# Stacking the low part of the attention's queries twice in a diffusion block on one core

## The chip, the cores and the metric

The kernel runs on one core of one Trainium2 chip. The metric is the device time of one execution in microseconds. Three runs of the kernel before took 866.24, 866.44 and 866.78 us; the median, 866.44 us, is the time that the prediction starts from.

## The reference

One layer of a hybrid backbone block is computed in float32 for 512 latent tokens (a grid of 8 rows by 64 columns), 256 context tokens and a model width of 1024. One combined projection feeds four mixers (pooling, Fourier, Hyena, neighbourhood attention), each 256 channels wide; their outputs are projected, gated, summed and projected again, and a gated feed-forward part follows. The change touches the scores of the neighbourhood attention alone:

```python
    s_nb = jnp.einsum('brqhd,brikhd->bhrqik', q, kb).astype(jnp.float32) * scale + bias
    s_cx = jnp.einsum('brqhd,bchd->bhrqc', q, kc).astype(jnp.float32) * scale
    ...
    s = jnp.concatenate([s_nb.reshape(B, NA_HEADS, rows, GRID_W, n_nb), s_cx], axis=-1)
    prob = jax.nn.softmax(s, axis=-1).astype(v.dtype)
```

There are 4 heads of 64 channels. A query sees a window of 8 rows by 16 columns of the grid and all 256 context keys.

## The kernel before

Everything lies with channels on the 128 partitions and tokens on the free axis, save in the attention. Nearly all products run in a one-pass float32 format of TensorE (F32R) that keeps fewer bits; so that no accuracy is lost, each operand is split into a high part and a low part (`split`, lines 95 to 97: ACT copies to the high part, DVE subtracts it from the original for the low part), and a product is the sum of three matmuls, high by high, high by low, low by high (`mm3`, lines 99 to 102). Weights arrive by DMA from the SP queue in chunks and are split the same way (`load_split`, line 84).

The attention (lines 846 to 931) goes by units. A unit is one block of 16 columns (128 queries) of one head; there are 16 of them, u = 0 to 15. `scores` (line 852) runs the score products of a unit into two PSUM tiles, `psl` (neighbourhood keys, 256 or 384 columns) and `psc` (256 context keys), and has the softmax done by DVE and ACT: DVE adds the bias and takes the maxima (`sl`, `mx`), ACT takes exponentials (`pr`), DVE scales `pr`. `turn` (line 884), one unit later, transposes `pr` on TensorE (PSUM tiles `ptl`, `ptc`), and `values` (line 897), for two units together in every second one, multiplies by v (PSUM tile `pav`). The PSUM tiles named `psl`, `psc`, `ptl`, `ptc`, `pav` and `ppool` share four buffers under one tag (`ps`, line 74). Between the units runs `step` (line 915), one of the 24 merge steps of the other three branches: 24 matmuls of 512 columns for the gate (`pin`), 6 for the branch (`pbr`), one split of a weight chunk (`wgh` on ACT, `wgl` on DVE) and a sum on DVE (`sg`, `macc`). `mod_rest` (line 839) adds work for DVE alone (`wm`), fed by a DMA into two buffers.

The operands of the scores are built by `stack` (line 714), once for heads 0 and 1 ahead of the pooling branch, and once for heads 2 and 3 from inside `scores`. A head has 64 channels, half of the array's 128 rows. `stack` puts the high part of q into both halves of `qs`, and the high and the low part of k into the two halves of `ks` (and `kcs` for the context keys). One matmul of all 128 rows so gives high by high plus high by low. The third product, low part of q by high part of k, takes a second matmul, of the 64 rows that `own` names: lines 865 and 867.

The program text is not the order on an engine: the framework's planner orders the instructions of each engine ahead of time by its own estimate of their costs, except in a stretch at the start that is pinned. Each engine then runs its list in that order.

Of the kernel before, what the change touches and what calls it, by code (L numbers as in the profile page):

```python
# [8 lines left out]
F32 = mybir.dt.float32  # L9
# [37 lines left out]
def block_kernel(ctx: ExitStack, tc: tile.TileContext, A):  # L47
# [3 lines left out]
    # an engine whose instructions keep the program's order while pinned is set  # L51
# [104 lines left out]
    # the same, spread over the partitions (tokens on the free dimension)  # L156
# [9 lines left out]
    # the table of the square root, loaded ahead of its use  # L166
# [18 lines left out]
    with ExitStack() as mix:  # L185
# [22 lines left out]
        # =================== start: modulation, first norm, filters of hyena ===================  # L208
# [6 lines left out]
        with ExitStack() as st:  # L215
# [19 lines left out]
            # filters of hyena: the two sine layers  # L235
# [28 lines left out]
            # statistics of x: sums of squares on the tensor engine  # L264
# [19 lines left out]
            # sums and differences of the filters' two directions, for each t mod 4  # L284
# [3 lines left out]
            # the sum of both directions' magnitudes is the larger magnitude of their sum and difference  # L288
# [9 lines left out]
            def filt_abs(s):  # L298
                ab = vx[1 + s % 2]
                if s == 0:  # L300
                    V.tensor_tensor(hacc, ab[:, 0], ab[:, 1], ALU.max)
                    # the backward filter starts at the second tap
                    f0, f1 = hyp_[0:1, 0], hym_[0:1, 0]
                    G.tensor_tensor(f0, f0, f1, ALU.add)
                    G.tensor_scalar(f0, f0, 0.5, None, ALU.mult)
                    G.tensor_copy(f1, f0)
                else:
                    V.tensor_tensor(ab[:, 0], ab[:, 0], ab[:, 1], ALU.max)
                    V.tensor_add(hacc, hacc, ab[:, 0])
# [3 lines left out]
            # transform at the odd frequencies f < 128; from sums over t = 4 u + r for each r follow those of  # L313
            # f, 511 - f, 255 - f and 256 + f (the second and third with the sine part negated)
            def fold(j):
                if j == 0:
                    kst.extend(yslot("kst", dt=F32) for _ in range(4))
                kP, kM, kQ, kR = kst
                if j < 2:
                    src = (hyp_, hym_)[j]  # L320
                    pa, pb = ps("pKe"), ps("pKo")
                    for dst, q in ((pb, 2), (pa, 0)):
                        PE.matmul(dst, tabK[:, q, j], src[:, q], start=True, stop=True)
                    ob = sp.tile([P, T], F32, name="kob", tag="hm", bufs=3)
                    S.copy(ob, pb)
                    kpa[j] = pa, ob
                else:
                    # tabK's last part is that of t mod 4 = 3 negated
                    src, cs, q, dst = ((hyp_, 0, 3, kQ[:, 0]), (hym_, 1, 3, kQ[:, 1]),
                                       (hyp_, 1, 4, kR[:, 0]), (hym_, 0, 4, kR[:, 1]))[j - 2]  # L330
                    pa = ps("pKe")
                    PE.matmul(pa, tabK[:, 1, cs], src[:, 1], start=True, stop=False)
                    PE.matmul(pa, tabK[:, q, cs], src[:, 3], start=False, stop=True)
                    S.copy(dst, pa)
# [6 lines left out]
            # shift and scale of the first norm, channel tile by channel tile, for c and c_ctx  # L341
# [175 lines left out]
        # =================== input projection, hyena ===================  # L517
# [9 lines left out]
        # projections that run while hyena's transforms occupy the vector engine  # L527
# [23 lines left out]
        # v with tokens on the partitions, for x in blocks of 16 columns  # L551
# [48 lines left out]
        # one order of hyena: to the spectrum, product, first stage back  # L600
        def spectrum(o, z):
# [16 lines left out]
            # cosine and sine sums for each t mod 4, then those of the four frequencies that share them  # L618
# [21 lines left out]
            # product of the spectra  # L640
# [6 lines left out]
            # back: coefficients of cos and sin for t mod 4 = 0, 2, 1, 3  # L647
# [13 lines left out]
        # back to the tokens, skip, gate  # L661
# [49 lines left out]
        # q's high part twice, k's high and low part, one above the other: one pass has both products  # L711
        stacks = []

        def stack(ct):
            ql = ap_.tile([P, T], F32R, name="ql", tag="ql", bufs=1)
            for o in range(2):
                own, other = slice(o * 64, o * 64 + 64), slice(64 - o * 64, 128 - o * 64)
                qs = ap_.tile([P, T], F32R, name="qs", tag="qs", bufs=2)
                ks = ap_.tile([P, T], F32R, name="ks", tag="ks", bufs=2)
                kcs = ap_.tile([P, TC], F32R, name="kcs", tag="kcs", bufs=2)  # L720
                split(qs[own], ql[own], qt[own, ct])
                S.copy(qs[other], qt[own, ct])
                for st, src in ((ks, kt), (kcs, kc)):
                    S.copy(st[own], src[own, ct])
                    V.tensor_sub(st[other], src[own, ct], st[own].bitcast(F32))
                stacks.append((qs, ql[own], ks.rearrange("p (r x) -> p r x", r=8), kcs, own))

        # bias of each head, in the three forms that the columns' windows take
# [18 lines left out]
        # =================== pooling over windows of 2, 4 (first tile) and 8, 16 (second tile) ===================  # L747
# [5 lines left out]
        for c in range(2):  # L753
# [5 lines left out]
            # entry t of a sum over a window w covers t - w/2 .. t + w/2 - 1  # L759
# [19 lines left out]
        # =================== fnet ===================  # L779
        bd = yslot("bd", (P, TC), F32)  # L780
        nc.sync.dma_start(bd, A["bd"])
        # sums and differences of the tokens t and T - t, for even and odd t
# [10 lines left out]
        for e in range(2):  # L793
            tabF.append(xtile("tabF").rearrange("p (c k) -> p c k", c=2))
            nc.sync.dma_start(tabF[e], A["tabF"][:, e])
            p = ps("pucs")
            for c in range(2):
                for cs in range(2):
                    o = slice(c * TC + cs * P, c * TC + (cs + 1) * P)
                    PE.matmul(p[:, o], uft[:, c, 2 * e + cs], bd[:, cs * P:(cs + 1) * P], start=True, stop=e == 1 or cs == 0)  # L800
                    if e == 0 and cs == 1:
                        # the token T / 2, which has no partner, in the place of the sine part of t = 0
                        PE.matmul(p[:, o], mid[:, c], bd[:, 0:P], start=False, stop=True)
            ucs.append(xtile("ucs"))
            S.copy(ucs[e], p)
        yh_fn, yl_fn = yslot("yfh"), yslot("yfl")
        for c in range(2):
# [5 lines left out]
            # the even part plus and minus the odd part  # L813
# [6 lines left out]
        # =================== q, k, v, context ===================  # L820
        macc = [xtile("macc") for _ in range(KT)]

        def merge(b, jt, y):
            wh, wl = load_split(A["wg"][b * KT + jt], WCH, name="wg")
            p = projw(wh, wl)
            # a gate's sigmoid is (1 + tanh(x / 2)) / 2; the half goes into the sum's scale
# [12 lines left out]
        def mod_rest(t):  # L839
            # one column block of the modulation's other parts  # L840
            wm = mrp.tile([P, D], F32, name="wm2", tag="wm2", bufs=2)
            nc.sync.dma_start(wm, A["wmB"][t])
            V.tensor_tensor_reduce(wm, wm, cb, 1.0, 0.0, ALU.mult, ALU.add, modc[:, t:t + 1])


        # =================== attention, fnet, pooling, merge of the first branches ===================
        with at:
# [3 lines left out]
            # scores, their maximum, exponentials and sum  # L851
            def scores(ct, i, o):
# [8 lines left out]
                qs, ql, ks, kcs, own = stacks[h]  # L861
# [3 lines left out]
                PE.matmul(plv, ql[:, qc], ks[own, :, kw], start=False, stop=True)  # L865
                PE.matmul(pc[:, :TC], qs[:, qc], kcs, start=True, stop=False)
                PE.matmul(pc[:, :TC], ql[:, qc], kcs[own], start=False, stop=True)
# [15 lines left out]
            # keys on the partitions  # L883
# [12 lines left out]
            # product with v, two heads at a time  # L896
# [37 lines left out]
        # =================== last branch, merged sum ===================  # L934
# [11 lines left out]
        # =================== output projection ===================  # L946
# [28 lines left out]
        # the last tiles in halves of the tokens, so that the second norm starts ahead of their end  # L975
# [17 lines left out]
    # =================== feed-forward ===================  # L993
    with ExitStack() as ff:
# [25 lines left out]
        # the first tiles in halves of the tokens, two at a time  # L1020
# [191 lines left out]
```

## Time and profile before

| | |
|---|---|
| median of three runs | 866.44 us |
| span of the profiled execution | 864.0 us |
| TensorE matmuls busy | 843.5 us (98%) |
| TensorE weight loads busy | 685.5 us (79%) |
| DVE busy | 501.2 us (58%) |
| ACT busy | 333.1 us (39%) |
| POOL busy | 6.0 us (1%) |

The span runs from the first to the last instruction of one execution; 2.4 us of the median lie outside it. PE stands for TensorE's matmuls and PEld for its weight loads, which are instructions of their own. The ends of matmuls are modelled and overlap with the next ones, so a busy share says little of how fast the work goes: the distance from the start of one matmul to the start of the next does. In the rows below a row of the timeline gives start, length, engine, line, operation, output and inputs, the shape (rows of the array by columns of the array, then the moving operand), the count of merged instructions, and in brackets the idle time of the engine ahead of it with what ended it. Every line reads L60, because all instructions go through one helper there; the tiles' names tell them apart.

### The profile page before, as it was taken

The numbers are of one execution on the slowest core, as the hardware profiler recorded it, in microseconds if no ns is written. First come the engines' busy times: TensorE is split into PE (matmuls) and PEld (weight loads), VectorE is DVE, ScalarE is ACT, GpSimd is POOL, SyncE is SP. The second block draws the span as 40 slices with busy tenths as digits, with TensorE's granted clock in tenths as the row PEclk, the third lists the DMA queues.
The fourth block names the chain that finished last, engine by engine and source line by source line (L and its number), as shares of the span: only waits on it lengthen the run. The fifth ranks groups of instructions, "written<-read, shape, count | busy, mean of one in ns | idle before, by whom it ended". The sixth has DMA issues, their size and how long they took to land.

```text
span 864.0 us, 10732 instructions
## 1 busy us (share of the span) xinstructions
PE 843.5 (98%) x4192; PEld 685.5 (79%) x4192; DVE 501.2 (58%) x870; ACT 333.1 (39%) x519; POOL 6.0 (1%) x16
## 2 busy tenths in 40 slices
PE   6999999989999999999999999999999999999996
PEld 2577889777777778888888998888888888888886
DVE  4879997698797773444444774444444444233233
ACT  7544452625453342323333363333333333232321
POOL 0100000000000000000000000000000000000000
PEclk9999999999999999999999999999999999999998
DMA  8912214545555532223332222222222223223222
GB/s 315 414 50 74 98 43 162 164 168 180 195 183 183 199 137 92 91 92 116 124 126 98 73 89 108 98 98 98 98 98 98 98 94 95 86 92 91 86 68 98
DMA packets 30362, 107.30 MB, mean 124 GB/s; under 512 B 3783, under 2 KB 4935, under 8 KB 29288
## 3 DMA queue, kind: packets, MB, share of 16 engines
q1 hardware_dynamic: 30312, 106.62, 35.2%
q8 instruction: 33, 0.54, 0.2%
q14 instruction: 17, 0.14, 0.0%
HBM read 104.51 MB, written 2.10 MB: 123 GB/s over the span
## 4 chain that ended last, share of the span: by engine, by line
PE 86%; DVE 8%; ACT 2%; DMA 2%; issue 1%; SPq 0%; DVEq 0%; ACTq 0%
PE pup L60 28%; PE pin L60 25%; PE pdn L60 14%; PE pwo L60 5%; PE pbr L60 5%; PE psc L60 1%; DVE za L60 1%; PE pav L60 1%; PE pKe L60 1%; PE psl L60 1%; DVE winl L60 1%; DVE zb L60 1%; PE ptl L60 1%; DMA cb<-in_crow_dram 1%; PE pmod L60 1%
## 5 line engine op out<-in xcount | busy, mean ns | idle before, releaser
L60 PE MATMUL pup<-hxh,wupl 128*128 128x512 f32 (+1 forms) x376 | 140.8, 376 | 0.0
L60 PE MATMUL pup<-hxl,wuph 128*128 128x512 f32 (+1 forms) x376 | 140.6, 376 | 0.0
L60 PE MATMUL pup<-hxh,wuph 128*128 128x512 f32 (+1 forms) x376 | 139.9, 376 | 0.7 <-ACT wuph L60 0.4
L60 PE MATMUL pdn<-act,wdnh 128*128 128x512 f32 (+1 forms) x396 | 112.7, 368 | 0.0
L60 PE MATMUL pin<-hxh,wgh 128*128 128x512 f32 x256 | 101.4, 396 | 0.6 <-ACT wgh L60 0.6
L60 PE MATMUL pin<-hxh,wgl 128*128 128x512 f32 x256 | 100.5, 393 | 0.0
L60 PE MATMUL pin<-hxl,wgh 128*128 128x512 f32 x256 | 100.3, 392 | 0.0
L60 DVE TENSOR_TENSOR wupl<-wupr,wuph 128x1024 fp32r<-128x1024 f32 x44 | 53.9, 1225 | 71.5 <-ACT wuph L60 69.7
L60 ACT CAST wuph<-wupr 128x1024 fp32r<-128x1024 f32 x44 | 46.3, 1053 | 92.3 <-PE pup L60 86.3
L60 PEld LDWEIGHTS pdn<-act,wdnh 128*128 128x128 f32 x396 | 71.6, 189 | 12.0
L60 PEld LDWEIGHTS pup<-hxh,wuph 128*128 128x128 f32 x376 | 70.1, 188 | 13.8 <-ACT wuph L60 0.6
L60 PEld LDWEIGHTS pup<-hxh,wupl 128*128 128x128 f32 x376 | 70.7, 188 | 12.9 <-DVE wupl L60 0.2
L60 PEld LDWEIGHTS pup<-hxl,wuph 128*128 128x128 f32 x376 | 70.6, 188 | 12.9
L60 PE MATMUL pdn<-act,wdnl 128*128 128x512 f32 (+1 forms) x198 | 72.4, 366 | 0.0
L60 ACT ACTIVATE sg<-pin 128x512 f32<-128x512 f32 x32 | 19.2, 600 | 119.5 <-PE pin L60 119.5
L60 DVE TENSOR_TENSOR wdnl<-wdnr,wdnh 128x1024 fp32r<-128x1024 f32 (+1 forms) x24 | 27.2, 1134 | 63.2 <-ACT wdnh L60 63.1
L60 DVE SCALAR_TENSOR_TENSOR sg<-sg,pbr 128x512 f32<-128x512 f32 x24 | 16.5, 688 | 80.2 <-PE pbr L60 80.2
L60 PEld LDWEIGHTS pin<-hxh,wgh 128*128 128x128 f32 x256 | 48.1, 188 | 10.8 <-ACT wgh L60 1.0
L60 PEld LDWEIGHTS pin<-hxh,wgl 128*128 128x128 f32 x256 | 48.1, 188 | 10.5 <-issue 0.5
L60 PEld LDWEIGHTS pin<-hxl,wgh 128*128 128x128 f32 x256 | 48.1, 188 | 10.1 <-issue 0.5
L60 PE MATMUL pin<-hxh,winh 128*128 128x512 f32 x128 | 51.7, 404 | 0.0
L60 ACT CAST wdnh<-wdnr 128x1024 fp32r<-128x1024 f32 (+1 forms) x24 | 23.6, 982 | 72.4 <-PE pdn L60 66.7
(265 smaller groups left out, 1429.2 us busy)
## 6 DMA issues: line engine op xcount, KB each, us to landing
wupr<-in_wup_dram SPq DMA_DIRECT2D x44, 512.0 KB, 3.4
wgr<-in_wg_dram SPq DMA_DIRECT2D x32, 640.0 KB, 3.8
wm<-in_wmB_dram SPq DMA_DIRECT2D x32, 512.0 KB, 4.7
wm<-in_wmA_dram SPq DMA_DIRECT2D x8, 1024.0 KB, 10.7
winr<-in_win_dram SPq DMA_DIRECT2D x16, 512.0 KB, 3.5
wdnr<-in_wdn_dram SPq DMA_DIRECT2D x16, 512.0 KB, 3.4
wor<-in_wout_dram SPq DMA_DIRECT2D x8, 512.0 KB, 3.5
wdnr<-in_wdn_dram SPq DMA_DIRECT2D x8, 384.0 KB, 3.0
```

What stands on the lines that cost most here:

```text
L60: ins = f(*a, **k)
```

## The change

The low part of q becomes a tile like `qs`: a buffer for each head (two under the tag `ql` where there was one for a pair of heads), with the low part in both halves. `stack` makes two subtractions for a head where it made one; the copies on ACT stay two. The second product of each pair takes all 128 rows of `ql` and of `ks` (or `kcs`), where it took 64. It thereby also adds the product of the two low parts, which was left out before. Columns, counts of matmuls and everything else stay. (The diff also empties comment lines, which are left out here.)

```diff
         def stack(ct):
-            ql = ap_.tile([P, T], F32R, name="ql", tag="ql", bufs=1)
             for o in range(2):
                 own, other = slice(o * 64, o * 64 + 64), slice(64 - o * 64, 128 - o * 64)
                 qs = ap_.tile([P, T], F32R, name="qs", tag="qs", bufs=2)
+                ql = ap_.tile([P, T], F32R, name="ql", tag="ql", bufs=2)
                 ks = ap_.tile([P, T], F32R, name="ks", tag="ks", bufs=2)
                 kcs = ap_.tile([P, TC], F32R, name="kcs", tag="kcs", bufs=2)
-                split(qs[own], ql[own], qt[own, ct])
-                S.copy(qs[other], qt[own, ct])
+                for part in (own, other):
+                    S.copy(qs[part], qt[own, ct])
+                    V.tensor_sub(ql[part], qt[own, ct], qs[own].bitcast(F32))
                 for st, src in ((ks, kt), (kcs, kc)):
                     S.copy(st[own], src[own, ct])
                     V.tensor_sub(st[other], src[own, ct], st[own].bitcast(F32))
-                stacks.append((qs, ql[own], ks.rearrange("p (r x) -> p r x", r=8), kcs, own))
+                stacks.append((qs, ql, ks.rearrange("p (r x) -> p r x", r=8), kcs))
...
-                qs, ql, ks, kcs, own = stacks[h]
+                qs, ql, ks, kcs = stacks[h]
                 qc, kw = slice(i * P, (i + 1) * P), slice(j0 * 16, (j1 + 1) * 16)
                 plv = pl[:, :n].rearrange("p (r x) -> p r x", r=8)
                 PE.matmul(plv, qs[:, qc], ks[:, :, kw], start=True, stop=False)
-                PE.matmul(plv, ql[:, qc], ks[own, :, kw], start=False, stop=True)
+                PE.matmul(plv, ql[:, qc], ks[:, :, kw], start=False, stop=True)
                 PE.matmul(pc[:, :TC], qs[:, qc], kcs, start=True, stop=False)
-                PE.matmul(pc[:, :TC], ql[:, qc], kcs[own], start=False, stop=True)
+                PE.matmul(pc[:, :TC], ql[:, qc], kcs, start=False, stop=True)
```

## Rows read from the trace of the kernel before

**Rows 1.** The page: its heading, and each engine's busy time, share and instructions.
```profile
span 864.0 us, 10732 instructions
PE 843.5 (98%) x4192; PEld 685.5 (79%) x4192; DVE 501.2 (58%) x870; ACT 333.1 (39%) x519; POOL 6.0 (1%) x16
```

**Rows 2.** Windows: stretch, its length, busy time by engine, granted clock, DMA share, GB/s.
```profile
200.00:257.00 57.00, 57.00 (x294) 43.60 (x292) 47.64 (x121) 29.51 (x67) 0.00 (x0) 1.00 0.49 167
257.00:320.00 63.00, 63.00 (x318) 49.19 (x319) 48.21 (x117) 23.72 (x52) 0.00 (x0) 1.00 0.55 187
350.00:413.00 63.00, 63.00 (x280) 52.16 (x279) 26.83 (x30) 19.04 (x22) 0.00 (x0) 1.00 0.32 113
```

**Rows 3.** Timeline of PE around unit 9, from the last branch matmul to `pav`.
```profile
264.63 0.39 PE L60 MATMUL pbr<-yph,wgl 128*128 128x512 f32 x1
264.86 0.28 PE L60 MATMUL psl<-ks,qs 128*128 128x256 f32 x1
265.07 0.38 PE L60 MATMUL psl<-ks,ql 64*128 64x256 f32 x1
265.38 0.38 PE L60 MATMUL psc<-kcs,qs 128*128 128x256 f32 x1
265.69 0.38 PE L60 MATMUL psc<-kcs,ql 64*128 64x256 f32 x1
266.00 0.44 PE L60 MATMUL ptl<-ident,pr 128*128 128x128 f32 x2
266.28 0.38 PE L60 MATMUL ptc<-ident,pr 128*128 128x128 f32 x2
...
267.06 0.66 PE L60 MATMUL pav<-pt,vt 128*64 128x128 f32 x8
```

**Rows 4.** Timeline of PEld in the same unit.
```profile
264.63 0.19 PEld L60 LDWEIGHTS psl<-ks,qs 128*128 128x128 f32 x1
265.07 0.18 PEld L60 LDWEIGHTS psl<-ks,ql 64*128 64x128 f32 x1 [0.24 <-issue]
```

**Rows 5.** Timeline of PE in a run of 256-column matmuls, all of 128 rows.
```profile
150.65 0.28 PE L60 MATMUL pvc<-hch,winh 128*128 128x256 f32 x1
150.77 0.28 PE L60 MATMUL pvc<-hcl,winh 128*128 128x256 f32 x1
```

**Rows 6.** Instructions of the tile `ql`: ns minimum/median/maximum, first and last start, forms.
```profile
L60 PE MATMUL psl<-ks,ql x16: 382/410/446, 197.3 to 320.8; 64*128 64x256 f32 x8, 64*128 64x384 f32 x8
...
L60 PE MATMUL psc<-kcs,ql x16: 378/380/384, 197.9 to 321.4; 64*128 64x256 f32 x16
L60 DVE TENSOR_TENSOR ql<-qt,qs x4: 674/686/690, 165.1 to 249.6; 64x512 fp32r<-64x512 f32 x4
```

**Rows 7.** Timeline of DVE during the first `stack`, and of PE behind it.
```profile
165.10 0.68 DVE L60 TENSOR_TENSOR ql<-qt,qs 64x512 fp32r<-64x512 f32 x1 [0.19 <-ACT qs L60]
166.37 0.69 DVE L60 TENSOR_TENSOR ks<-kt,ks 64x512 fp32r<-64x512 f32 x1 [0.59 <-ACT ks L60]
...
168.60 0.69 DVE L60 TENSOR_TENSOR ks<-kt,ks 64x512 fp32r<-64x512 f32 x1 [0.48 <-ACT ks L60]
...
174.74 0.50 PE L60 MATMUL ppool<-dh,pbs 128*128 128x512 f32 x1 [1.25 <-ACT dh L60]
```

**Rows 8.** Timeline of DVE and PE through unit 7.
```profile
237.66 1.23 DVE L60 CUSTOM_DVE_ANT_0 wm<-wm,cb 128x1024 f32<-128x1024 f32 x1 [2.73 <-DMA wm<-in_wmB_dram]
...
246.44 0.28 PE L60 MATMUL psl<-ks,qs 128*128 128x256 f32 x1
...
247.82 0.42 DVE L60 CUSTOM_DVE_ANT_0 sl<-psl,bias 128x256 f32<-128x256 f32 x1
...
248.65 0.55 PE L60 MATMUL pav<-pt,vt 128*64 128x128 f32 x6
```

**Rows 9.** Timeline of DVE in unit 9.
```profile
265.13 0.69 DVE L60 SCALAR_TENSOR_TENSOR sg<-sg,pbr 128x512 f32<-128x512 f32 x1 [2.01 <-PE pbr L60]
```

**Rows 10.** Waits from 200 to 322 us: us in total, times, longest.
```profile
PEld psc L60 <- DVE pt L60: 0.2, 1, 0.2
```

## The prediction

> **What bounds the kernel now.** I read the page first [rows 1]: TensorE's matmuls are busy for 98% of the span of 864.0 us, DVE for 58%. Then the busy time by windows over the attention, 197 to 322 us [rows 2]: PE has no gap there, the granted clock is 1.00 (the 2.4 GHz level), and DVE is the only other engine with a heavy load, 47.6 of 57 us in the first half and 48.2 of 63 in the second. Behind the attention DVE falls to 26.8 of 63 us. So PE sets the pace, but the first half of the attention is the one place where DVE is near enough to take over.
>
> A busy PE is no PE at its best. In the timeline the distance between starts tells more. Inside a run of 256-column matmuls of 128 rows the next start comes after 0.12 us [rows 5]; behind a 512-column one after 0.23 us [rows 3] (264.63 to 264.86). In a unit of the attention the four score matmuls, 256 columns each, start at 264.86, 265.07, 265.38 and 265.69, and the transposes at 266.00 [rows 3]: 0.21, 0.31, 0.31 and 0.31 us, 1.14 us for what would take 0.48 at the plain pace. The weight loads show why [rows 4]: the load for the 128-row `qs` starts at 264.63, under the running `pbr` matmul, and is over when its turn comes. The load for the 64-row `ql` starts at 265.07, together with its own matmul, after an idle time of 0.24 us that is put down to "issue", no semaphore. Whenever the row count changes from 128 to 64 or back, the matmul ahead runs out and the load follows in the open.
>
> **What the change removes.** All 32 matmuls of 64 rows become 128-row ones of as many columns: 16 into `psl` and 16 into `psc` [rows 6], two a unit. Every instruction in the unit then has 128 rows, and no change of row count is left. Per unit the excess is 0.09 + 0.19 + 0.19 + 0.19 us (the four distances less 0.12). The 384-column units have the same excess against 0.17 us, which I interpolate between 0.12 for 256 columns and 0.23 for 512. That is 0.66 us. The first instruction behind the unit carries a tail of the last change: its two transposes of 128 columns take 0.28 us to the next group, and at no more than the 0.12 us of 256 columns each they would take 0.24, so the tail is at least 0.04; a full change, 0.19, is its other end. The transposes are nearer to the low end and I take 0.06, which makes 0.72 us in the 11 units with transposes behind the scores. In the first five a longer matmul stands there, for which I take the middle, 0.11, so 0.77. Sum: 11 x 0.72 + 5 x 0.77 = 11.8 us of PE time. Bounds: 16 x 0.70 = 11.2 and 16 x 0.85 = 13.6. The longer reduction costs no more: length goes by columns, as the distances of 128-row matmuls [rows 5] already show.
>
> Here a rule of the Trainium skill speaks against the change. The page "TensorE: Matmul & The Clock Gate", section "The mechanism" in its part 3, says that a weight load overlaps a running matmul only when the row groups differ. By it no 128-row load could hide under a 128-row matmul, and the exposed loads would stay. The load at 264.63 under the `pbr` matmul, both of 128 rows, shows that they do hide here [rows 3, 4]; I keep the rule as part of a rival.
>
> **What the change adds.** Four subtractions on DVE, one for each head, at 0.69 us [rows 6]: 2.8 us in all; on ACT nothing. They come in two places.
>
> *First `stack`.* Its DVE work leads without a gap into the pooling chain, and PE does wait for that chain: 1.25 us idle ahead of `ppool` at 174.74 [rows 7]. So 2 x 0.69 = 1.4 us could land on the path in full. But DVE itself waits there for ACT's copies, 0.59 us ahead of the first `ks` and 0.48 ahead of the second [rows 7], and the new subtraction needs only `qs[own]`, which is ready by then. It fills those waits: 0.69 - 0.59 = 0.1 and 0.69 - 0.48 = 0.2, together 0.3 us on the path. Bounds: 0 (the planner puts them behind the pooling) to 1.4.
>
> *Second `stack`, and DVE behind a faster PE.* This is the open term. In the first half (200 to 257 us) eight units would shorten by about 0.74 us each, so 57 becomes 51 us, and DVE's work grows to 47.6 + 1.4 = 49 us [rows 2]. That leaves 2 us for all of DVE's waits, which were 9.4, and one of them does not shrink with PE: 2.73 us for the DMA of `wm` at 237.66, which was started when DVE itself freed the buffer [rows 8]. What is late next: `pav`, because it takes the PSUM buffer that DVE frees by reading `sl` of the same unit. In unit 9 `pav` starts 267.06 - 264.86 = 2.2 us after the first score [rows 3]; with 0.72 us gone that is 1.5. DVE in that unit had waited 2.01 us for `pbr` at 265.13 [rows 9], takes 0.69 for `sg` and 0.42 for `sl`, so `sl` is out at about 1.3 us: just in time. In unit 7 DVE is late already: `sl` starts at 247.82 and ends at 248.24, 1.8 us after the score at 246.44 [rows 8], and `pav` would want to start at 1.5. Counted from the last point where DVE waited for PE (unit 5), PE arrives 1.4 us sooner by unit 7 while DVE's list between, with the DMA wait in it, is no shorter and holds up to two subtractions more. I take it that the gain of these two units, 1.4 us, is lost. In unit 3 the second score already waits a little for DVE's copy `pt` [rows 10]; as the scores move up by about 0.4 us, I count 0.4 us there, and 0.2 for the rest of the opening. Sum of this term: 2.0 us; bounds 0 (another order of DVE's list hides all) and 5.9 + 1.4 = 7.3 (the eight units gain nothing and the subtractions come on top).
>
> In the second half DVE has 63 - 48.2 = 14.8 us to spare against 8 x 0.72 = 5.8; its wait of 2.01 us in a unit falls to 1.3 and stays above zero. Behind the attention nothing else binds PE: the same merge steps run there without a gap at DVE 26.8 of 63 us [rows 2], so what PE gains is carried to the end. The two buffers of `ql` let the third head's low part start a unit earlier than one buffer did; I cost that at nothing. The clock is at its upper level all through and PE becomes denser, so it stays.
>
> **The sum.** Against the span: 864.0 - 11.8 + 0.3 + 2.0 = 854.5 us. The median lies 2.4 us above the span, for what is outside it, which the change doesn't touch: 866.4 - 9.5 = 856.9 us.
>
> **The rivals.**
> *Everything hides.* The planner, which orders by its own costs, may place the four subtractions so that neither `ppool` nor `pav` is late: 866.4 - 11.8 = 854.6, or 854.9 with the first 0.3 us. For it: the list of DVE in the second half has room. Against it: the 2 us left in the first half.
> *DVE becomes the bound of the first half.* If its waits stay as they are, the first eight units gain nothing: 866.4 - 8 x 0.72 + 0.3 + 1.4 = 862.3; with half of its waits kept, 49 + 4.7 = 53.7 against 51, a loss of 2.7 us, near 857.6. For it: the DMA's wait of 2.73 us stays [rows 8]. Against it: waits like the 2.01 us of [rows 9] are for PE, and come sooner with it.
> *The loads stay in the open.* If what costs 0.19 us isn't the change of row count but something that all score matmuls share, the starts stay 0.31 us apart: no gain, and 0.3 us from the first `stack`, 866.7. Against it: the `qs` loads behind a 128-row matmul hide.
> *Slower: DVE's subtractions alone reach PE.* With the loads in the open, nothing pays for them; all four on the path give 866.4 + 4 x 0.69 = 869.2. Their places are the first `stack`, ahead of `ppool` [rows 7], and unit 7, ahead of `pav` [rows 8]. It decides from 1.7 of these 2.8 us on.
>
> **How the numbers follow.** 1.7 us, 0.2%, is about what a measurement of this kernel can tell from no change. Forecast with its mis-sizings (855.5 to 859): 0.62. Everything hides (853.6 to 855.5): 0.22. DVE bound (859 to 862.5): 0.10. Loads in the open, within 0.2%: 0.03 (the rule on weight loads is part of that). Slower: 0.03. Faster is so 0.94. The range for 8 in 10 runs from 853.6 (0.8 us short of the 13.6 us bound with nothing added, as the transposes speak for the lower part of that term) to 860.8, inside the case of a DVE bound; the loss of 7.3 us lies beyond it.
>
> **What would show it.** In the changed kernel's timeline the four scores of a unit should start 0.12 us apart (0.17 for 384 columns), each load under the matmul ahead, and the "issue" waits of `psl` and `psc` loads should be gone. `ql` should have 8 subtractions. `ppool` should wait about 1.5 us. New PE waits should appear ahead of `pav` or `psc`, released by DVE, in the first half of the attention, about 2 us in all, and hardly any in the second. It is wrong if the scores still start 0.31 us apart, or if PE's waits for DVE come to 5 us or more.

## The result

The changed kernel takes 855.65 us, the median of four runs (855.23 to 856.96), against 866.34 us (864.58 to 866.78) for the kernel before on the same chip: a ratio of 0.9882, with a 95% interval of 0.9868 to 0.9897. It is 10.7 us faster; 9.5 us were forecast, and 855.65 lies inside the range. The profiled execution has a span of 853.4 us.

First the heading and the busy times of the page, to be read against [rows 1]:

```profile
span 853.4 us, 10736 instructions
PE 832.1 (97%) x4192; PEld 683.8 (80%) x4192; DVE 502.6 (59%) x874; ACT 332.1 (39%) x519; POOL 5.9 (1%) x16
```

There are four more instructions, all on DVE, and 11.4 us less of busy TensorE for the same 4192 matmuls. Next the timeline of PE in unit 9 (start, duration, operation, idle time before it and its releaser where there is one), which answers to [rows 3], and of its weight loads, which answers to [rows 4]:

```profile
258.23 0.39 PE L60 MATMUL pbr<-yph,wgl 128*128 128x512 f32 x1
258.46 0.28 PE L60 MATMUL psl<-ks,qs 128*128 128x256 f32 x1
258.58 0.28 PE L60 MATMUL psl<-ks,ql 128*128 128x256 f32 x1
258.69 0.28 PE L60 MATMUL psc<-kcs,qs 128*128 128x256 f32 x1
258.82 0.28 PE L60 MATMUL psc<-kcs,ql 128*128 128x256 f32 x1
258.94 0.38 PE L60 MATMUL ptl<-ident,pr 128*128 128x128 f32 x2
259.16 0.38 PE L60 MATMUL ptc<-ident,pr 128*128 128x128 f32 x2
259.93 0.66 PE L60 MATMUL pav<-pt,vt 128*64 128x128 f32 x8
```

```profile
258.24 0.19 PEld L60 LDWEIGHTS psl<-ks,qs 128*128 128x128 f32 x1
258.46 0.19 PEld L60 LDWEIGHTS psl<-ks,ql 128*128 128x128 f32 x1
258.58 0.19 PEld L60 LDWEIGHTS psc<-kcs,qs 128*128 128x128 f32 x1
```

The four scores start 0.12, 0.11, 0.13 and 0.12 us apart, where it was 0.21 and three times 0.31. From the first score to `ptc` it takes 0.70 us instead of 1.42. Each load now starts one matmul early: that for `ql` at 258.46, with the matmul of `qs`, and is over when its turn comes at 258.58. The waits of the weight loads over the attention, 195 to 312 us, say the same for all units (us in total, times, longest); before, from 200 to 322 us, the loads of `psl` and `psc` waited 3.7 us in 15 places and 1.6 us in 8 for "issue":

```profile
PEld pav L60 <- DVE mx L60: 2.6, 6, 1.0
...
PEld psc L60 <- issue: 0.3, 1, 0.3
...
PEld psl L60 <- issue: 0.2, 1, 0.2
```

The tile view of `ql` shows that all 32 products have 128 rows now and take 0.1 us less each, that DVE does eight subtractions, and that the price of one is unchanged [rows 6]:

```profile
L60 PE MATMUL psl<-ks,ql x16: 282/310/343, 196.7 to 310.0; 128*128 128x256 f32 x8, 128*128 128x384 f32 x8
...
L60 PE MATMUL psc<-kcs,ql x16: 281/283/286, 197.0 to 310.2; 128*128 128x256 f32 x16
L60 DVE TENSOR_TENSOR ql<-qt,qs x8: 673/685/690, 164.5 to 244.4; 64x512 fp32r<-64x512 f32 x8
```

What is left of DVE's price stands in two places. The first is the first `stack`, which answers to [rows 7]: DVE's subtractions, the `ks` that no longer waits, and the matmul behind.

```profile
164.51 1.38 DVE L60 TENSOR_TENSOR ql<-qt,qs 64x512 fp32r<-64x512 f32 x2 [0.19 <-ACT qs L60]
165.81 0.68 DVE L60 TENSOR_TENSOR ks<-kt,ks 64x512 fp32r<-64x512 f32 x1
...
168.15 0.68 DVE L60 TENSOR_TENSOR ks<-kt,ks 64x512 fp32r<-64x512 f32 x1
...
176.07 0.50 PE L60 MATMUL ppool<-dh,pbs 128*128 128x512 f32 x1 [1.37 <-ACT dh L60]
```

The second is unit 7, which answers to [rows 8]; the last line is the only wait of a PE matmul between 195 and 312 us:

```profile
233.29 1.22 DVE L60 CUSTOM_DVE_ANT_0 wm<-wm,cb 128x1024 f32<-128x1024 f32 x1 [2.93 <-DMA wm<-in_wmB_dram]
236.11 1.37 DVE L60 TENSOR_TENSOR ql<-qt,qs 64x512 fp32r<-64x512 f32 x2
...
240.75 1.22 DVE L60 CUSTOM_DVE_ANT_0 wm<-wm,cb 128x1024 f32<-128x1024 f32 x1
240.84 0.28 PE L60 MATMUL psl<-ks,qs 128*128 128x256 f32 x1
242.50 0.41 DVE L60 CUSTOM_DVE_ANT_0 sl<-psl,bias 128x256 f32<-128x256 f32 x1
242.98 0.88 PE L60 MATMUL pav<-pt,vt 128*64 128x128 f32 x12 [0.60 <-DVE mx L60]
```

Where the time went shows when the span is cut at matmuls that both kernels have. The table is worked out from start times in the timelines: of a pair of transposes of the values (`pvt`, near 154 us, some 10 us ahead of the first `stack`), the first score, the first output projection and the last transpose of the result.

| stretch, us | before | after | difference |
|---|---|---|---|
| start to that `pvt` | 154.6 | 154.0 | -0.6 |
| to the first score (first `stack`) | 42.3 | 42.5 | +0.2 |
| to the first output projection | 244.1 | 233.2 | -11.0 |
| to the last transpose | 415.6 | 415.7 | 0.0 |
| to the end | 7.3 | 8.2 | +0.9 |

The change touches the second and third stretch. The first and the last differ too, and are taken up below.

### The profile page after: what moved, and what is told of

Same layout as the page of the kernel before. It is cut to its first block, busy times and chain, and to the rows that moved or that the text cites. A ratio compares the mean times of both kernels' runs of the same rounds, so it can differ in the third digit from the quotient of the medians.

```text
span 853.4 us, 10736 instructions
## 1 busy us (share of the span) xinstructions
PE 832.1 (97%) x4192; PEld 683.8 (80%) x4192; DVE 502.6 (59%) x874; ACT 332.1 (39%) x519; POOL 5.9 (1%) x16
## 4 chain that ended last, share of the span: by engine, by line
PE 86%; DVE 8%; ACT 2%; DMA 1%; issue 1%; SPq 0%; DVEq 0%; ACTq 0%
PE pup L60 28%; PE pin L60 25%; PE pdn L60 14%; PE pwo L60 5%; PE pbr L60 5%; PE pss L60 1%; DVE za L60 1%; PE pKe L60 1%; PE pav L60 1%; DVE winl L60 1%; DVE zb L60 1%; PE pmod L60 1%; DMA cb<-in_crow_dram 1%; DMA wm<-in_wmB_dram 1%; DVE wgl L60 1%
```

## The experiments

**The changed kernel again.** Theory: the wait ahead of `pav` in unit 7 belongs to the planned order and comes back in each execution. Rival: it was chance. No edit.

> The changed kernel once more, without an edit, beside the three others. Theory (PE's own path from the first score to the first output projection, 233.2 us in the first profile, is fixed by the order of the instructions; the landing of an early DMA and the length of the last one vary by themselves): 233.1 to 233.3 us again on that path, 0.6 to 0.7 us of waiting ahead of pav in unit 7, and a median of 855 to 856.5 us. Rival (the wait in unit 7 is chance): a path of 232.5 us in this profile.

Measured: 855.70 us, ratio 0.988 [0.9865, 0.9895]. The wait ahead of `pav` in unit 7 is 0.69 us here and was 0.60 in the first profile, and the third stretch is 233.3 us. The wait is no chance; nor is the long tail (8.2 us).

**Without the four new subtractions.** Scores run as in the changed kernel, but the other half of `ql` is filled with zeros by GpSimd. So the product of the low query with the keys' other part is left out.

```diff
-                for part in (own, other):
-                    S.copy(qs[part], qt[own, ct])
-                    V.tensor_sub(ql[part], qt[own, ct], qs[own].bitcast(F32))
+                split(qs[own], ql[own], qt[own, ct])
+                S.copy(qs[other], qt[own, ct])
+                G.memset(ql[other].bitcast(F32), 0.0)
```

> The changed kernel, but the second half of ql is set to zero by POOL, so that DVE makes four subtractions in place of eight and the product of the two low parts is left out. Theory (the gain is the row count alone; the four added subtractions are nearly hidden): the scores start 0.12 us apart as in the changed kernel; at most the 0.7 us that pav waits in unit 7 comes back, so 855.0 to 855.7 us. Rival (the added subtractions take about 2 us of the gain, as the prediction had it): 853.5 to 854 us.

Measured: 854.46 us, ratio 0.9866 [0.9853, 0.988]. The third stretch takes 232.6 us, 11.6 less than before: this is the gain of the scores with nothing set against it, and against the 233.2 of the changed kernel it puts the price of the second `stack` at 0.6 us. The median lies between the two expected ranges: beside the 0.6 us, its profile has a tail of 7.3 us in place of 8.2 (taken up below) and a start that is 1.0 us longer. But its unit 7 is instructive (timeline of DVE and PE):

```profile
241.63 0.28 PE L60 MATMUL psl<-ks,qs 128*128 128x256 f32 x1
...
243.19 0.88 PE L60 MATMUL pav<-pt,vt 128*64 128x128 f32 x12
...
243.57 0.42 DVE L60 CUSTOM_DVE_ANT_0 sl<-psl,bias 128x256 f32<-128x256 f32 x1
```

`sl` starts 1.94 us behind the score, later than the 1.66 of the changed kernel, and still `pav` does not wait: it starts 0.38 us ahead of `sl`, so here it cannot have been given the buffer that `sl` frees (its weight load is released by ACT's `pt`, not by DVE). This run shows what the wait costs, but not that a shorter list on DVE is what removes it. The run with DVE kept free, below, tests that.

**The subtractions alone.** The stacked `ql` is made, but the scores use only its own 64 rows, as before.

```diff
...
-                PE.matmul(plv, ql[:, qc], ks[:, :, kw], start=False, stop=True)
+                PE.matmul(plv, ql[own, qc], ks[own, :, kw], start=False, stop=True)
...
-                PE.matmul(pc[:, :TC], ql[:, qc], kcs, start=False, stop=True)
+                PE.matmul(pc[:, :TC], ql[own, qc], kcs[own], start=False, stop=True)
```

> The additions alone: ql is built as in the changed kernel, with eight subtractions and a buffer for each head, but the second products still take the 64 rows of own. Theory: within 0.5 us of the kernel before, 865.8 to 866.9 us, with the scores 0.31 us apart, as PE is slow enough in each unit to cover DVE. Rival (the subtractions are on the path: 0.3 us at the first stack, up to 2.8 us in all): 866.7 to 869.2 us.

Measured: 866.92 us, ratio 1.0009 [1.0, 1.0018]. The scores of unit 9 start 0.31 us apart again, and the third stretch is 244.2 us, that of the kernel before: behind the slower PE the second `stack` costs nothing. The first `stack` costs 0.14 us with or without the faster scores. By its median alone, 0.7 us above the kernel before, this run would fall to the rival; by the stretches it doesn't: of the 0.7 us that its span is longer, 0.14 are the first `stack`'s and 0.9 the tail's (8.2 us, taken up below), while the start is 0.35 shorter. So the gain is all in the scores' row count, and what DVE takes back appears only once PE is faster.

**The change of row count by itself.** In the kernel before, the two 128-row scores are put first, then the two 64-row ones: two changes of row count a unit instead of four, with no other work added or removed. One line moves:

```diff
                 PE.matmul(plv, qs[:, qc], ks[:, :, kw], start=True, stop=False)
+                PE.matmul(pc[:, :TC], qs[:, qc], kcs, start=True, stop=False)
                 PE.matmul(plv, ql[:, qc], ks[own, :, kw], start=False, stop=True)
-                PE.matmul(pc[:, :TC], qs[:, qc], kcs, start=True, stop=False)
                 PE.matmul(pc[:, :TC], ql[:, qc], kcs[own], start=False, stop=True)
```

> The kernel before with one line moved: both 128-row products of a unit come first, then both 64-row products, so that the row count changes twice in a unit and not four times; all 32 products stay at 64 rows. Theory (each change of row count costs about 0.19 us, not the 64 rows): the second 64-row load hides under the first 64-row matmul; 16 x 2 x 0.19 = 6.1 us less, about 860.2 us. Rival (a 64-row product is dear by itself, its load always in the open): no gain, 866.3 us.

Measured: 860.53 us, ratio 0.9937 [0.9925, 0.995], over half of the gain for one moved line. Timeline of PE in its unit 9:

```profile
261.81 0.28 PE L60 MATMUL psl<-ks,qs 128*128 128x256 f32 x1
261.93 0.28 PE L60 MATMUL psc<-kcs,qs 128*128 128x256 f32 x1
262.14 0.39 PE L60 MATMUL psl<-ks,ql 64*128 64x256 f32 x1
262.37 0.28 PE L60 MATMUL psc<-kcs,ql 64*128 64x256 f32 x1
262.57 0.44 PE L60 MATMUL ptl<-ident,pr 128*128 128x128 f32 x2
262.85 0.38 PE L60 MATMUL ptc<-ident,pr 128*128 128x128 f32 x2
```

The starts are 0.12, 0.21, 0.23 and 0.20 us apart, and the first score to `ptc` takes 1.04 us, between 1.42 and 0.70. The distance behind the matmul ahead of a change is 0.09 us longer (0.21 against 0.12), and that behind the first matmul after it 0.11 longer (0.23), since its load is in the open. The third stretch falls by 5.8 us. The Trainium skill says on its page "TensorEngine Tiling (Array Packing)", section "Key Properties", that changing the tiling mode drains the engine; the 0.09 us ahead of a change are in line with that, and the 0.11 us behind it come on top.

**One of the two products alone.** Only the scores against the context use all 128 rows; those against the window keep 64.

```diff
...
-                PE.matmul(plv, ql[:, qc], ks[:, :, kw], start=False, stop=True)
+                PE.matmul(plv, ql[own, qc], ks[own, :, kw], start=False, stop=True)
```

> The changed kernel, but only the context product (psc) takes 128 rows; the neighbourhood product (psl) stays at the 64 rows of own. Theory (each change of row count costs about 0.19 us): two changes a unit are left, and 16 x 2 x 0.19 = 6.1 us are gained, less about 0.2 for the subtractions, so about 860.4 us, with the two psc matmuls 0.12 us apart. Rival (the 64-row products cost unequally, the context one most): 857 us or less.

Measured: 860.40 us, ratio 0.9934 [0.9921, 0.9948]. The third stretch is 238.3 us, 5.8 less, the same as for grouping: half of the changes of row count, half of the gain, whichever half it is. In its unit 9 the first matmul after the change back to 128 rows is followed by another of 128 rows:

```profile
261.58 0.39 PE L60 MATMUL psc<-kcs,qs 128*128 128x256 f32 x1
261.80 0.28 PE L60 MATMUL psc<-kcs,ql 128*128 128x256 f32 x1
261.92 0.38 PE L60 MATMUL ptl<-ident,pr 128*128 128x128 f32 x2
```

The two start 0.22 us apart, as far as the two of 64 rows in the grouped kernel (0.23), and only the next distance is the plain 0.12. So the 0.23 us there is the price of standing behind a change, not of 64 rows. Two ways to take away two of four changes agree to 0.1 us in the median, which speaks for a price by the change and not by the tile or the operand.

**DVE kept free of other work.** The reductions over `wm` and the sums into `macc` are pinned to the program's order, so the planner can't put them between the units' own steps. Nothing is left out.

```diff
-            V.tensor_tensor_reduce(wm, wm, cb, 1.0, 0.0, ALU.mult, ALU.add, modc[:, t:t + 1])
+            tc.keep_in_program_order(V.tensor_tensor_reduce(wm, wm, cb, 1.0, 0.0, ALU.mult, ALU.add, modc[:, t:t + 1]))
...
-            V.scalar_tensor_tensor(macc[jt], sg, 1.0, pb, ALU.add, ALU.mult)
+            tc.keep_in_program_order(V.scalar_tensor_tensor(macc[jt], sg, 1.0, pb, ALU.add, ALU.mult))
...
-                V.tensor_add(macc[jt], macc[jt], sg)
+                tc.keep_in_program_order(V.tensor_add(macc[jt], macc[jt], sg))
```

> The changed kernel, but DVE's modulation reductions (wm) are held in the program's order behind the merge sums (macc), so that the planner can't pull them ahead into the first half of the attention. Theory (DVE, loaded with these reductions and waiting 2.9 us for one of their DMAs, is what delays pav in unit 7): the wait of 0.66 us ahead of pav goes and the time falls by 0.3 to 0.8 us, 854.9 to 855.4 us. Rival (pav waits for the score's own chain through sl and mx, whatever else DVE has): no change, 855.7 us, or slower by a few us where the reductions pile up behind the attention.

Measured: 854.88 us, ratio 0.987 [0.9856, 0.9883]. Windows (stretch, length, then PE, PEld, DVE, ACT and POOL busy, granted clock, DMA share, GB/s), first of the changed kernel, then of this one:

```profile
195.00:250.00 55.00, 54.40 (x307) 45.15 (x306) 48.94 (x125) 30.13 (x68) 0.00 (x0) 1.00 0.56 188
...
320.00:440.00 120.00, 120.00 (x541) 99.09 (x540) 53.07 (x63) 36.70 (x45) 0.00 (x0) 1.00 0.33 109
```

```profile
195.00:250.00 55.00, 55.00 (x309) 45.80 (x309) 37.38 (x102) 30.60 (x68) 0.00 (x0) 1.00 0.28 92
...
320.00:440.00 120.00, 120.00 (x540) 98.75 (x540) 75.07 (x102) 36.41 (x44) 0.00 (x0) 1.00 0.58 188
```

11.6 us of DVE work, and half of the DMA traffic, leave the first half of the attention; behind the attention, where DVE has room, it is 22.0 us busier, with what left the second half. PE has no gap left in the first window, and its third stretch is 232.6 us with all the work in it. Its unit 7:

```profile
241.99 0.42 DVE L60 CUSTOM_DVE_ANT_0 sl<-psl,bias 128x256 f32<-128x256 f32 x1
...
242.59 0.88 PE L60 MATMUL pav<-pt,vt 128*64 128x128 f32 x12
242.59 0.53 PEld L60 LDWEIGHTS pav<-pt,vt 128*64 128x64 f32 x10 [0.36 <-DVE mx L60]
```

The first score of this unit starts at 241.11. `sl` follows after 0.88 us instead of 1.66, and the matmul of `pav` behind it doesn't wait. Its weight load is still released by DVE's `mx`, as in the changed kernel, so the same dependency holds and only its time has moved. This is the run that shows the cause: DVE's list, and not the subtractions as such, made `pav` late. It is also the best kernel here that computes everything, 0.8 us below the changed one by the medians; their intervals overlap (0.9856 to 0.9883 against 0.9865 to 0.9895 for the changed kernel run again), and in its profile the tail is 0.9 us shorter too, so 0.6 us of it are the wait's and not all.

**Both at once.** Zeros in `ql` and DVE's other work pinned; the same product is left out as above.

> Both reliefs of DVE at once: the second half of ql set to zero by POOL (the product of the two low parts is left out), and the modulation reductions held behind the merge sums. Theory (both take away the same wait of 0.66 us ahead of pav, so they don't add up): 232.5 us from the first score to the first output projection, and 854.5 to 855.1 us. Rival (each has a gain of its own): 853.6 to 854.2 us.

Measured: 854.46 us, ratio 0.9865 [0.9852, 0.9878], with a third stretch of 232.6 us. The two don't add up: after either, PE has no wait left in the attention, and the stretch is the same 232.6 us.

**The subtractions doubled.** Each of the eight is done twice, 16 in all.

```diff
                     V.tensor_sub(ql[part], qt[own, ct], qs[own].bitcast(F32))
+                    V.tensor_sub(ql[part], qt[own, ct], qs[own].bitcast(F32))
```

> The changed kernel with each subtraction into ql made twice, 16 in all: 2.8 us more of DVE work at the first stack and 2.8 us more at the second. Theory (the change's own additions were cheap because they filled DVE's waits for ACT and PE ran on; those waits are now used up and DVE's list ahead of unit 7 has no room left): PE waits 1 to 2 us more ahead of pav in unit 7, and with up to 2 us more ahead of ppool the time is 857 to 859.5 us. Rival (DVE has room for much more): within 0.7 us of the changed kernel, 855 to 856.4 us.

Measured: 859.37 us (858.14 to 861.36), ratio 0.9921 [0.9907, 0.9935], 3.7 us above the changed kernel timed beside it. Three of PE's waits from 156 to 325 us:

```profile
PE ppool L60 <- ACT dh L60: 2.9, 2, 1.7
...
PE pav L60 <- DVE mx L60: 1.1, 1, 1.1
...
PE ppool L60 <- DVE dl L60: 0.9, 1, 0.9
```

The second stretch grows by 4.2 us, the third by 0.8. In this profile the granted clock averages 0.57 between 156 and 160 us, near the 1.2 GHz level, behind a wait of 1.9 us of PE for `vb`; so up to 4 x 0.43 = 1.7 of the 4.2 us may be the clock's, and the other 2.5 are close to the 4 x 0.69 = 2.8 us that DVE got on top there. The two quickest executions, whose mean granted clock (0.996 and 0.997) is that of the changed kernel, took 858.14 and 858.20 us: 2.5 us above it as well. The change's own two subtractions cost 0.15 us in that place because they fill waits of DVE; more of them find none and land on the path. The wait at `pav`, which was expected to grow by 1 to 2 us in unit 7, moved to unit 9 and grew by 0.5; in unit 7 the load of `pav` is now released by ACT's `pt`, as in the run with zeros.

**The tail.** The end of the changed kernel is 0.9 us longer, though nothing in it was edited. In the DMA view of the last six us the changed kernel has one packet that the kernel before has not, a fetch of instructions while the result is written. First its queue (packets, MB, share), then what the DMA engines moved in these six us, in 40 slices, for the changed kernel and for the kernel before:

```profile
q14 instruction: 1, 0.01, 0.3%
GB/s 0 0 0 0 0 0 0 191 410 437 410 328 382 437 410 437 383 382 410 382 410 464 382 410 273 0 27 0 27 27 27 0 0 0 0 0 0 0 0 0
```

```profile
GB/s 0 0 0 0 0 0 0 0 0 0 0 0 0 410 437 410 410 382 410 437 410 382 437 410 437 382 328 410 410 410 82 0 0 0 0 0 0 0 0 0
```

Before, the output ends at once; after, the bulk ends and single packets follow (27 GB/s is one packet of 4096 bytes in a slice of 0.15 us). The last output transfer lands 4.15 us after its issue instead of 3.26: the 0.9 us lie in this transfer and nowhere else in the tail.

The theory was that the change's four DVE instructions moved this fetch into the output, and that it costs the 0.9 us. Three kernels were made to move it, and a fourth to split one of them. Eight small copies behind the feed-forward's activations, with a new tile as their target:

```diff
         act = []
+        pad = fp.tile([P, 1], F32, name="pad")
...
+            if f < 8:
+                V.tensor_copy(pad, gt[:, 0:1])
```

> The changed kernel with eight copies of one column on DVE added in the feed-forward part, where DVE is less than half busy; they compute nothing that is used. In the profiles the last transpose lies 8.18 us ahead of the span's end in four kernels, the changed one among them, and 7.28 us in the six others; in just those four a block of instructions is fetched by DMA 2.8 us ahead of the end, amid the output's DMA. Theory (that fetch delays the output, and when it falls depends on the number of instructions alone): with eight more the fetch leaves that place, the tail is 7.3 us and the time 854.6 to 855.1 us. Rival (the tail has another cause in the changed kernel): 8.2 us, and 855.5 to 855.9 us.

Measured: 857.46 us, ratio 0.9895 [0.988, 0.991]. The tail is 7.3 us and the fetch is not in the last 14 us, but the fourth stretch is 1.8 us longer (417.4), and the kernel is slower than the changed one. The same with four copies (`f < 4`) in the kernel before, which then has as many DVE instructions as the changed one:

> The kernel before with four such copies on DVE in the feed-forward part. Theory (a fetch of instructions amid the output's DMA): with as many DVE instructions as the changed kernel the fetch moves from behind the end to 2.8 us ahead of it, the tail grows from 7.3 to 8.2 us and the time by 0.9 us, to about 867.0 us. Rival: tail 7.3 us and no change, 866.1 us.

Measured: 867.98 us, ratio 1.0024 [1.0015, 1.0033]. Neither expected time came. The tail stayed at 7.3 us: the number of DVE instructions alone does not put the fetch into the tail, and that part of the theory fell. The 1.8 us on the fourth stretch came again (417.5 us). Next the eight copies with no new tile, into a column that is already there:

```diff
+            if f < 8:
+                V.tensor_copy(invc[:, 0:1], gt[:, 0:1])
```

> As the kernel with eight copies before it, but the copies go into a column of a tile that is there already and no longer used (invc), so that no tile moves in memory. Theory (a fetch of instructions amid the output's DMA made the changed kernel's tail 0.9 us longer; the slower down projection of that other kernel came from the shifted tiles): tail 7.3 us, 415.6 us from the first output projection to the last transpose, and 854.6 to 855.1 us. Rival (the copies themselves cost): 417.4 us on that stretch and 857 us.

Measured: 855.94 us, ratio 0.9879 [0.9864, 0.9893]. The tail is 7.3 us, no fetch falls into the last 14 us, and the fourth stretch is back at 415.6. But the median did not fall: in this profile the start takes 155.2 us instead of 154.0, and the wait at `pav` 1.1 us instead of 0.6. And the new tile with a single fill and no copies:

```diff
+        pad = fp.tile([P, 1], F32, name="pad")
+        G.memset(pad, 0.0)
```

> The changed kernel with the one-column tile in the feed-forward pool, written once by POOL, and no copies: every tile allocated behind it, the operands of the down projection among them, lies a little further on. Theory (the place of the operands in memory costs 1.8 us of PE time there): 417.4 us from the first output projection to the last transpose, matmuls of the down projection 4 ns further apart, and 857.3 to 857.7 us. Rival (the eight copies had cost it): 415.6 us, and 855.5 to 855.9 us.

Measured: 857.56 us, ratio 0.9895 [0.9879, 0.9912]. Tail 8.2 us with a fetch in it, fourth stretch 417.5 us. So the copies shorten the tail, with the tile or without it, and the tile alone makes the fourth stretch longer. One step of the chain of work that ended last, the down projection (start, us, engine, tile, instructions), in the changed kernel and with the tile:

```profile
798.43 14.99 PE pdn L60 x66
```

```profile
800.89 15.30 PE pdn L60 x66
```

The same 66 matmuls take 0.3 us longer. So do, by 0.25 to 0.33 us, the first seven of the ten steps of this stage; the last three do not.

## Why the prediction was right, step by step

**The bound.** PE sets the pace, and the clock is granted in full through the attention (1.00 in every window). Right: the scores' saving reaches the end, since the fourth stretch is the same to 0.1 us.

**The scores, -11.8 us.** Measured 11.6, from the run without the added subtractions (244.1 to 232.6), inside the bounds of 11.2 to 13.6. A unit with transposes behind its scores was put at 0.72 us and took 1.42 - 0.70 = 0.72. The plain pace of 0.12 us was the right goal, and the small tail in the transposes was there: their two groups start 0.22 us apart instead of 0.28. That a load of 128 rows hides under a matmul of 128 rows, which the prediction held against the rule of the Trainium skill's page "TensorE: Matmul & The Clock Gate", section "The mechanism", is shown by every score of the new unit: the load at 258.46 starts with the matmul of the same rows.

**The first `stack`, +0.3 us.** Measured +0.15, and 0.14 with the subtractions alone. The waits of 0.59 and 0.48 us ahead of `ks` are gone, as said, and `ppool` waits 1.37 us where about 1.5 were named. In DVE's list the price stands directly: from the first subtraction to the pooling chain it takes 4.69 us instead of 4.55. The planner also put eight more gate matmuls ahead of `ppool`, which the prediction did not foresee, so the two waits do not compare at the same place of PE's list.

**The second `stack` and DVE behind a faster PE, +2.0 us.** This is the term that was mis-sized: it measured 0.6. The place and the mechanism were right in unit 7: the wait for the DMA of `wm` stayed (2.93 us), `sl` starts 1.66 us behind the score, and `pav` waits for it. But the prediction held DVE's list of before fixed and added the subtractions to it. From the second score unit to the ninth DVE was busy 47.19 us in the kernel before (200.1 to 256.4) and 46.73 in the changed one (198.8 to 250.7), though two subtractions were added. The planner had made room: ahead of `sl` in unit 7 it used to do two reductions over `wm` in a row (244.93 and 246.07, 1.22 us each), and now does one; in the whole stretch `wm` takes DVE 12.78 us instead of 14.39. So 0.6 us of the 1.4 stayed, and the 0.4 us in unit 3 and 0.2 in the opening did not come at all: from the first score to that of unit 7 it takes 44.40 us here and 44.37 in the run without the added subtractions.

**The second half.** DVE's wait for `pbr` in unit 9 was to fall from 2.01 to about 1.3 us and fell to 1.54. No matmul waits there, as said.

**What the sum left out.** Two stretches that the change does not touch differ in the profiled executions by -0.6 us (start) and +0.9 us (tail). They are of the size of the forecast's error: the profile gives -11.6 + 0.6 + 0.15 = -10.85 us for what the prediction spoke of, and -10.85 - 0.6 + 0.9 = -10.55 for the span, which fell from 864.0 to 853.4. The start varies by more than the change moves it: over the 14 profiles here, before and after among them, it takes 153.7 to 156.1 us. Between these two kernels the difference is that of one DMA, which landed `cb` 6.03 us after its issue before and 5.22 after: ACT waits for it for 1.90 and 1.09 us, and PE behind ACT, ahead of that `pvt`, for 1.20 and 0.39. Why the DMA's time varies was not tried. And the 2.4 us outside the span were the median of three executions less the span of one: within one execution of the changed kernel it is 855.23 - 853.4 = 1.8 us, and within one of the kernel before, timed beside a later experiment, 866.12 - 864.2 = 1.9. So the base of the sum, 866.4 for a span of 864.0, was about 0.5 us high, which made the forecast slower by as much.

**The rivals.** "Everything hides" was given 854.6 to 854.9; the run with DVE's other work pinned came to 854.88 with the whole computation. The result lies at the line between that case (up to 855.5) and the forecast; that it fell on the forecast's side is luck, as the four executions spread from 855.23 to 856.96 us and the tail alone adds 0.9. "DVE becomes the bound of the first half" is out: that half shrank from 56.3 to 51.8 us. "The loads stay in the open" is out by the scores' starts, and the slower case with it: the subtractions alone add 0.66 us to the median and not 2.8.

## What to carry to other kernels

On an engine that is busy all through, read the distances between starts, not the durations: a matmul whose row count differs from its neighbour's paid about 0.2 us here, more than another 256-column matmul (0.12 us) would have taken. Where padding the operand to full rows is dear, grouping the matmuls of equal row count gets half of it by moving a line. And a planner's list is no constant: work that is added to a second engine displaces other work, so what it costs is found by holding the other work back, as pinning did here.

## What the runs showed of the hardware

A change between 128 and 64 rows costs in two parts, 0.09 us on the matmul of 256 columns ahead of it and 0.10 to 0.11 us on the one behind it. The second part is the same for either row count: the first two matmuls behind a change start 0.23 us apart at 64 rows (the grouped kernel) and 0.22 at 128 (the context product alone). No unit has more than two matmuls of 64 rows in a row, so their plain pace is not shown.

One extra tile of one column slowed matmuls that do not touch it: steps of the down projection took 15.30 us instead of 14.99, and the fourth stretch 1.8 us more in the three kernels that have the tile (417.4 to 417.5 us against 415.6 to 415.9), in one of them with no copies into it. That it is the place in memory of the tiles allocated behind it is inferred from the allocation's order, not shown; which address decides was not tried.

A fetch of instructions lay among the output's transfers in each of the kernels with a tail of 8.2 us (the changed kernel and its repeat, the subtractions alone, the context product alone, the tile alone), and in none of those with 7.3 us. In these five the last output transfer landed 4.15 to 4.17 us after its issue, in the nine others 3.24 to 3.28. Eight DVE instructions more moved the fetch away twice; pinning, with no instruction more, did so too. So in the profiled executions the 0.9 us go with the fetch. That the median falls without it is not shown: the two that should have fallen moved by +0.2 us (the eight copies with no new tile) and -0.1 us (tile and copies against the tile alone).
